# Output weights fetched ahead into lent ring places, convolution sums among the last projections, and triangular inverses by blocks of 64

## The chip, the cores and the metric

One core of one Trainium2 chip runs the kernel. The metric is the time of one execution on the device, in microseconds (us); the time before is the median of three runs, 1175.84 us (1175.05 to 1176.33). The engines are called PE (TensorE), PEld (its weight loads), DVE (VectorE), ACT (ScalarE), POOL (GpSimd) and SP (SyncE, which issues the loads).

## The reference

256 tokens of width 1024 go through two blocks. The first (Fourier mixing, neighbourhood attention, a gated merge and an MLP) is not touched. The second mixes three branches into one output projection and ends in 16 experts:

```python
h = rms_norm_2(x, norm_mix_g)
q, pc, pr = jnp.split(h @ w_in, ...)
o_att  = memory_cross_attention(q, mem_n, w_mk, w_mv)       # 256 wide
o_conv = conformer_conv(pc, conv_w, ...)                    # 384 wide, 31 taps in depth
o_rwkv = rwkv7_bidirectional(pr, ...)                       # 384 wide, 6 heads of 64
x = x + jnp.concatenate([o_att, o_conv, o_rwkv], -1) @ w_out
x = x + expert_choice_ffn(rms_norm_2(x, norm_ffn_g), w_router, w_e_gate, w_e_up, w_e_down)
return rms_norm_2(x, final_norm_g)

# each head, in both directions of time:
state = state * w_t + (state @ -kk_t) (kk_t * a_t)^T + v_t k_t^T
y_t   = state @ r_t
```

Each expert takes the 32 tokens of its highest gates. Its three matrices are 1024 x 1024 in float32, so the experts read 16 x 3 x 4 MB = 201 MB.

## The kernel before

**Block 2's branches** (`branches`) follow the last products of block 1. The input projections come first (`pw` <- `hmh`, `hml`: the activations as a high and a low half, times weights that ACT and DVE turn into a high and a low half, `split`). A projection piece is loaded by `wload` into a `raw` tile, split by `wsplit`, and multiplied by the generator that `dense_steps` returns.

**The recurrence without a scan.** The 256 steps are cut into two chunks of 128. `first_scores` and `other_scores` make each chunk's score matrices (`psab` on PE, masked into `LM` on DVE; `prh` and `py` carry the chunk's own values), for each direction twelve (6 heads, 2 chunks), held as three tiles `i` of four matrices `z`. A triangular system of 128 unknowns must then be inverted. `blocks16` inverts the 16x16 blocks on its diagonal (`prep` on PE, `g` and `Gc` on DVE, 15 rounds) and writes them into a 128x128 matrix `Gm`. `levels` doubles the blocks: 16 to 32, 32 to 64, and 64 to 128. A level needs the transposed inverse `Tm` (by `turn`: `pt`, copied by ACT), `pp` = score matrix times `Tm` (masked by DVE into `P`, in the last level copied by ACT), and `pg` = `P` times `Gm` (copied by ACT, in the last level by DVE). In the first two levels each of these is a 128x128 matmul with blocks of zeros in it; in the last it is 64x64, of one quadrant. `finish` then solves with the inverse (`pu`, `pzz`, `prz`, `py`). All of it is done for direction 0 and direction 1; direction 1's `blocks16` is woven among direction 0's levels.

**The convolution.** Two thirds of the channels are summed by DVE (`cacc`, one operation a tap). The last third is summed on PE: for each of the 31 taps ACT writes a scaled copy `cp` and PE adds it in with an identity (`pconv`, `conv_pe`). `conv` ends with the norm over channels (`pm` <- `cacc`, `aa`; a square root on ACT, RECIPROCAL on DVE, a sigmoid on ACT) and writes the high and low outputs `oc`. The memory attention's outputs are `om`, the recurrence's `orw`.

**The output projection** (`out_proj`) is cut by rows: `op` multiplies the 640 rows for attention and convolution by pieces of 256 columns, `second` the 384 rows for the recurrence by pieces of 512 columns, both added to `x`. The products of `op` are handed out by count among the steps of `finish(1)` (`OPB`) and of the tail behind it.

**The tail** norms the recurrence's output: `pm` <- `ysum`, squares, `pkk`, a square root, RECIPROCAL, `pbk`, products with the gate (`kds`), and at last `orw`.

**The ring.** The experts' weights go through places in SBUF in the order in which they are used (gate, up, down of expert 0, 1, ...): narrow places of 1 MB and wide ones of 2 MB. Places are added as memory comes free (`ring_room`), and `ring_load` issues into those that are free; `E1` says how many loads go where. Two of the last places serve for something else before: one as a `split` tile, one as `orw`.

**What sets the order.** Generators are woven by hand (`weave`, with the counts `W`), but each instruction recorded is then placed in its engine's queue by a scheduler, which may move it ahead of or behind others where nothing depends on it. `in_turn` holds it to the order of recording; all loads of block 2 on SP are held so. Each engine works its queue in order, so an instruction that waits holds up all behind it.

## Time and profile before

| | |
|---|---|
| median of 3 runs | 1175.84 us |
| the profiled execution | 1172.29 us, its span 1170.5 us |
| PE busy | 1046.5 us (89%) |
| DVE busy | 508.1 us (43%) |
| ACT busy | 418.2 us (36%) |
| DMA | 313.86 MB, 268 GB/s over the span |

The table is of one profiled execution; the median is of other runs. A share over the whole span is a mean over stages. Up to some 450 us block 1 runs, from there to 716 us block 2's branches, then the router and the experts. In the second part of the page the DMA row is at 9 (90% or more) from about 700 us to the end, with 426 to 428 GB/s, and at 0 to 4 before it; PE is at 9 up to there and at 7 to 8 behind. For a float32 matmul of the program the trace shows two on PE (8 in a level step of four matrices), for one on split halves (`pw`) one.

### The profile page before, as it was taken

What the parts mean: (1) busy time and instruction counts of PE and PEld (TensorE: products, weight loads), DVE (VectorE), ACT (ScalarE), POOL (GpSimd) and SP (SyncE); (2) the same over time, 40 slices, a digit from 0 to 9 for tenths busy, and PEclk for the clock granted to TensorE, in tenths of its full rate; (3) what the DMA queues carried; (4) which work ended last, traced back from release to release, by engine and by line L of the source; (5) the groups of instructions that cost most, each with busy time, mean ns of one, the idle gap of its engine ahead of it and who ended that gap; (6) DMA issues with size and microseconds to landing.
All of it is one profiled execution on the core that took longest, in us unless ns stands there. A gap on an engine that the chain in (4) does not pass through costs nothing.

```text
span 1170.5 us, 19106 instructions
## 1 busy us (share of the span) xinstructions
PE 1046.5 (89%) x8188; PEld 754.2 (64%) x8188; DVE 508.1 (43%) x964; ACT 418.2 (36%) x718; POOL 44.4 (4%) x50
## 2 busy tenths in 40 slices
PE   5999999999999999999899998989877777777775
PEld 4886676899999999898678887434332222222222
DVE  3544356587555555659997545212111111111102
ACT  4542368656444444676434534101100000000003
POOL 0000000021000000101210002000000000000000
PEclk9999999999999999999999998999988988998888
DMA  9974545545555553530401469999999999999996
GB/s 349 365 287 165 180 165 210 181 182 179 213 180 180 183 185 120 175 109 1 180 1 46 153 235 372 361 419 370 426 427 428 426 425 427 428 426 425 427 427 286
DMA packets 34964, 313.86 MB, mean 268 GB/s; under 512 B 4800, under 2 KB 5568, under 8 KB 9152
## 3 DMA queue, kind: packets, MB, share of 16 engines
q1 hardware_dynamic: 34880, 312.65, 67.2%
q8 instruction: 64, 1.05, 0.4%
q14 instruction: 20, 0.16, 0.0%
HBM read 311.59 MB, written 1.05 MB: 267 GB/s over the span
## 4 chain that ended last, share of the span: by engine, by line
PE 70%; DMA 20%; DVE 5%; ACT 3%; issue 1%; POOL 1%; SPq 0%; ACTq 0%; POOLq 0%; DVEq 0%
PE pw L299 22%; DMA ew<-in_w_e_up_dram 13%; PE pd L299 9%; PE acc L299 9%; DMA ew<-in_w_e_down_dram 6%; PE pgu L299 5%; PE pada L299 2%; PE pv L299 2%; PE pqf L299 2%; PE psab L299 2%; PE pg L299 1%; PE pconv L299 1%; PE pp L299 1%; PE py L299 1%; PE prep L299 1%; DMA raw<-in_w_branch_gate_dram 1%
## 5 line engine op out<-in xcount | busy, mean ns | idle before, releaser
L284 DVE TENSOR_TENSOR split<-raw,split 128x1024 fp32r<-128x1024 f32 (+2 forms) x148 | 176.8, 1203 | 114.2 <-ACT split L278 113.5
L299 PE MATMUL pgu<-ew,XE 128*32 128x256 f32 x2048 | 145.4, 427 | 57.2 <-DMA ew<-in_w_e_up_dram 56.0
L278 ACT ACTIVATE split<-raw 128x1024 fp32r<-128x1024 f32 (+2 forms) x148 | 151.9, 1033 | 123.8 <-PE pw L299 65.1
L299 PE MATMUL pd<-ew,hidT 128*32 128x512 f32 (+2 forms) x560 | 149.4, 572 | 12.4 <-DVE hidT L2137 6.2
L299 PEld LDWEIGHTS pgu<-ew,XE 128*32 128x32 f32 x2048 | 67.5, 120 | 127.3 <-DMA ew<-in_w_e_up_dram 68.9
L299 PEld LDWEIGHTS pd<-ew,hidT 128*32 128x32 f32 x560 | 40.5, 111 | 110.5 <-issue 97.3
L299 PE MATMUL acc<-uh,split 128*128 128x256 f32 x512 | 94.7, 283 | 0.0
L299 PE MATMUL pw<-h2h,split 128*128 128x256 f32 x512 | 92.9, 280 | 0.0
L296 DVE SCALAR_TENSOR_TENSOR hid<-pgu,rs,hid 128x256 f32<-128x256 f32 x16 | 7.7, 484 | 189.7 <-ACT hid L275 189.7
L296 DVE SCALAR_TENSOR_TENSOR ye<-pd,ig,ye 128x512 fp32r<-128x512 f32 (+2 forms) x35 | 24.6, 704 | 144.1 <-ACT ye L275 142.5
L275 ACT ACTIVATE hid<-pgu,rs 128x256 f32<-128x256 f32 x16 | 7.6, 474 | 215.0 <-PE pgu L299 215.0
L275 ACT ACTIVATE ye<-pd,ig 128x512 fp32r<-128x512 f32 (+2 forms) x35 | 22.8, 651 | 164.7 <-PE pd L299 164.6
L299 PEld LDWEIGHTS acc<-uh,split 128*128 128x128 f32 x512 | 80.8, 192 | 0.0
L299 PEld LDWEIGHTS pw<-h2h,split 128*128 128x128 f32 x512 | 79.3, 188 | 0.0
L299 PE MATMUL acc<-ul,split 128*128 128x256 f32 x256 | 72.5, 283 | 0.0
L299 PE MATMUL pw<-h2l,split 128*128 128x256 f32 x256 | 71.4, 279 | 0.0
L299 PE MATMUL pw<-hxh,split 128*128 128x256 f32 x320 | 61.6, 286 | 0.1
L299 PE MATMUL pw<-hmh,split 128*128 128x256 f32 x320 | 61.0, 288 | 0.0
L299 PEld LDWEIGHTS pw<-hxh,split 128*128 128x128 f32 x320 | 50.0, 188 | 9.5 <-issue 8.1
L299 PEld LDWEIGHTS pw<-hmh,split 128*128 128x128 f32 x320 | 50.5, 191 | 1.6 <-PE pz L299 0.5
L299 PEld LDWEIGHTS acc<-ul,split 128*128 128x128 f32 x256 | 49.0, 191 | 0.2 <-DVE ul L284 0.2
L299 PEld LDWEIGHTS pw<-h2l,split 128*128 128x128 f32 x256 | 48.0, 187 | 0.0
(441 smaller groups left out, 1734.0 us busy)
## 6 DMA issues: line engine op xcount, KB each, us to landing
ew<-in_w_e_up_dram SPq DMA_DIRECT2D x28, 2048.0 KB, 18.5
ew<-in_w_e_down_dram SPq DMA_DIRECT2D x28, 2048.0 KB, 19.1
ew<-in_w_e_gate_dram SPq DMA_DIRECT2D x27, 2048.0 KB, 22.5
raw<-in_w_mlp_dram SPq DMA_DIRECT2D x32, 1024.0 KB, 4.8
raw<-in_w_ada_dram SPq DMA_DIRECT2D x24, 1024.0 KB, 5.5
raw<-in_w_in_dram SPq DMA_DIRECT2D x18, 1024.0 KB, 5.7
ew<-in_w_e_gate_dram SPq DMA_DIRECT2D x10, 1024.0 KB, 12.9
raw<-in_w_branch_gate_dram SPq DMA_DIRECT2D x8, 1024.0 KB, 4.9
```

Of the source, the lines that this page charges most:

```text
L275: self.nc.scalar.activation(out, in_, func, **kw)
L278: self.nc.scalar.activation(out, in_, AF.Copy)
L284: self.nc.vector.tensor_tensor(out=out, in0=a, in1=b, op=op)
L296: self.nc.vector.scalar_tensor_tensor(out=out, in0=a, scalar=s, in1=b, op0=op0, op1=op1)
L299: self.nc.tensor.matmul(out, lhsT, rhs, start=start, stop=stop, **kw)
```

## The change

- `conv_pe` is made before the last projections and is handed out there: 4 taps among the last products and 8 after the first of the last steps, its copies in a tile of another pool.
- `Gm` and `Tm` hold the two 64x64 diagonal blocks, stacked over 128 partitions (128 x 4 x 64), instead of a 128x128 matrix. The levels 16 to 32 and 32 to 64 multiply 64x64 blocks on two diagonal quadrants of PE. The transposed inverse comes from its own product, `pt` = `P` times `Gm` the other way round, instead of a transposition of `pg`. Only before the last level is the inverse written out whole (`G`), with zeros by POOL.
- The 640 rows' pieces of `w_out` are loaded in one go as soon as memory is there: two into the two `raw` tiles, two into one lent wide ring place; the 384 rows' two pieces into another lent place. The first lent place goes back to the ring when `orw` is placed, the second when the output products are done. `E1` is gone; the ring loads what has room.
- The first pieces are split before direction 1's second level, and one step of `op` follows each of the last eight steps of that level and the last one.

```diff
 OPB = 5, 5, 5, 5, 0
-E1 = 4, 2, 2, 0
 PRE = 0
...
     out = []
+    def halves(m):
+        return np.concatenate([m[0:64, 0:64], m[64:128, 64:128]])
     for d in range(2):
...
             m = (r // (2 * n) == c // (2 * n)) & ((r // n) % 2 == 1) & ((c // n) % 2 == 0)
-            out.append(m | (s == t))
+            out.append(halves(m | (s == t)))
+    out.append(halves(s // 16 == t // 16))
     out.append(s // 16 == t // 16)
...
-    def wload(self, name, r0, r1, c0, c1, k=None):
-        wp, tag = self.raws[0]
-        self.raws = self.raws[1:] + self.raws[:1]
-        raw = wp.tile([128, 2048], F32, tag=tag, name="raw", bufs=1)
+    def wload(self, name, r0, r1, c0, c1, k=None, raw=None):
         src = self.wsrc(name, r0, r1, c0, c1)
+        if raw is None:
+            wp, tag = self.raws[0]
+            self.raws = self.raws[1:] + self.raws[:1]
+            raw = wp.tile([128, 2048], F32, tag=tag, name="raw", bufs=1)
         view = raw[:, 0:src.shape[1]]
...
                 self.branches(x2, hi, lo, ob)
-            self.ring_load()
             self.ring_room(RING2)
...
                     self.logits(x2, 2 * n - 2)
+            self.free.append(self.lent)
+            self.ring_load()
             with self.in_turn("PE"):
...
-    def out_proj(self, x, ob, h, between=0):
+    def out_proj(self, x, ob, h, piece):
...
         o = tuple(Tiles(lambda k, z=z: ob[a + k][:, z]) for z in range(2))
-        return self.dense_steps("w_out_2", 0, 1024, b - a, [o], [ev], preload=2, fine=not h,
-                                between=between and partial(self.ring_load, between), r0=a * 128)
+        return self.dense_steps("w_out_2", 0, 1024, b - a, [o], [ev], fine=not h, r0=a * 128, piece=piece)
...
+        cw = self.v("conv_w_2").rearrange("p (k i) -> p k i", k=31)
+        cacc = rb.tile([128, 3, 256], F32, name="cacc")
+        def conv_pe():
+            ps = self.pst("pconv")
+            for t in range(31):
+                p_ = self.sq.tile([128, 2, 256], F32, name="cp", tag="sq", bufs=2)[:, t % 2]
+                self.act(p_, u[:, 2, t:t + 256], AF.Copy, scale=cw[:, t, 2:3])
+                self.mm(ps[:, 0:256], self.ident, p_, t == 0, t == 30)
+                yield
+            self.act(cacc[:, 2], ps[:, 0:256], AF.Identity, bias=self.v("conv_b_2", 2))
+        cpe = conv_pe()
         dec, ky, s0, s1 = decays(), keys(), start(0), start(1)
...
         for g in (dec, cd, cd, dec, cd, ma, cd, dec, cd, ma, cd, None, prd, dec, prd, ma, prd, dec, prd, ma,
-                  ky, prd, ma, ky, s0, prd, s0, s0, prd, ma, s1, prd, s1, s1):
+                  ky, prd, ma, ky, s0, prd, s0, s0, prd, *[cpe] * 4, ma, s1, prd, *[cpe] * 8, s1, s1):
             if g is None:
...
         mst = [cr[:, 512 + d * 256:512 + (d + 1) * 256].rearrange("p (y t) -> p y t", y=2) for d in range(2)]
-        lev = [[cr[:, 1024 + (d * 2 + n) * 128:1024 + (d * 2 + n + 1) * 128] for n in range(2)] for d in range(2)]
+        lev = [[cr[:, 1024 + (d * 2 + n) * 64:1024 + (d * 2 + n + 1) * 64] for n in range(2)] for d in range(2)]
         bm = cr[:, _CR["bm"]:_CR["bm"] + 128]
+        bmh = cr[:, _CR["bmh"]:_CR["bmh"] + 64]
         sel = wk2.tile([128, 2064], F32, name="sel")
...
-        def conv_pe():
...
-                p_ = wk2.tile([128, 256], F32, name="cp", tag="cp", bufs=2)
...
                [matrices(i) for i in range(3, 6)]]
-        gms = itertools.cycle([(wk if n in (1, 2, 3) else wk0).tile([128, 4, 128], F32, name="Gm%d" % n)
-                               for n in range(7)])
+        whole = [[p.tile([128, 4, 128], F32, name="G%d%d" % (d, n)) for n in range(3)] for d, p in enumerate((wk0, wk))]
+        gms = itertools.cycle([wk0.tile([128, 4, 64], F32, name="Gm%d" % n) for n in range(9)])
...
                 gm = G[d, i] = next(gms)
-                self.tt(gm.rearrange("p n (b c) -> p n b c", b=8),
-                        g[:, 4 * i:4 * i + 4, None, :].to_broadcast([128, 4, 8, 16]),
-                        bm.rearrange("p (b c) -> p b c", b=8)[:, None].to_broadcast([128, 4, 8, 16]), ALU.mult)
+                self.tt(gm.rearrange("p n (b c) -> p n b c", b=4),
+                        g[:, 4 * i:4 * i + 4, None, :].to_broadcast([128, 4, 4, 16]),
+                        bmh.rearrange("p (b c) -> p b c", b=4)[:, None].to_broadcast([128, 4, 4, 16]), ALU.mult)
             yield
-            turn(d)
+            for i in range(3):
+                turned(d, i, [self.ident[q, None, q].to_broadcast([64, 4, 64]) for q in hs])
             yield
+        hs = slice(0, 64), slice(64, 128)
         def v4(ps):
-            return ps.rearrange("p (n t) -> p n t", n=4)
-        def turn(d):
+            return ps[:, 0:256].rearrange("p (n t) -> p n t", n=4)
+        def turned(d, i, factors, which=hs):
+            ps = v4(self.pst("pt1", "pw"))
+            for z in range(4):
+                for q in which:
+                    self.mm(ps[q, z], G[d, i][q, z], factors[hs.index(q)][:, z], True, True)
+            T_[d, i] = wk0.tile([128, 4, 64], F32, tag="Tm", name="Tm", bufs=3)
+            for q in (which if len(which) == 1 else [slice(0, 128)]):
+                self.cpa(T_[d, i][q], ps[q])
+        def levels(d):
+            a, b = hs if d == 0 else hs[::-1]
             for i in range(3):
-                ps = v4(self.pst("pt1", "pw"))
-                for z in range(4):
-                    self.tr(ps[:, z], G[d, i][:, z])
-                T_[d, i] = wk0.tile([128, 4, 128], F32, tag="Tm", name="Tm", bufs=3)
-                self.cpa(T_[d, i], ps)
-        def levels(d):
+                nc.gpsimd.memset(whole[d][i][b, :, a], 0.0)
             for n in range(2):
-                ml = lev[d][n][:, None, :].to_broadcast([128, 4, 128])
+                ml = lev[d][n][:, None, :].to_broadcast([128, 4, 64])
                 p1 = []
...
                     for z in range(4):
-                        self.mm(ps[:, z], LM[d, i][:, 0, z], T_[d, i][:, z], True, True)
-                    t = wk0.tile([128, 4, 128], F32, tag="P1", name="P1", bufs=3)
+                        for q in hs:
+                            self.mm(ps[q, z], LM[d, i][q, 0, z, q], T_[d, i][q, z], True, True)
+                    t = wk0.tile([128, 4, 64], F32, tag="P1", name="P1", bufs=3)
                     p1.append(t)
...
                     for z in range(4):
-                        self.mm(ps[:, z], p1[i][:, z], G[d, i][:, z], True, True)
-                    G[d, i] = next(gms)
-                    self.cpa(G[d, i], ps)
+                        for q in hs:
+                            self.mm(ps[q, z], p1[i][q, z], G[d, i][q, z], True, True)
+                    turned(d, i, [p1[i][q] for q in hs], [a] if n else hs)
+                    if n == 0:
+                        G[d, i] = next(gms)
+                        self.cpa(G[d, i], ps)
+                    else:
+                        G[d, i] = whole[d][i]
+                        for q in hs:
+                            self.cpa(G[d, i][q, :, q], ps[q])
                     yield
-                turn(d)
-                yield
-            a, b = (slice(0, 64), slice(64, 128)) if d == 0 else (slice(64, 128), slice(0, 64))
             p1 = []
             for i in range(3):
-                ps = self.pst("pp1", "pw").rearrange("p (n t) -> p n t", t=64)
+                ps = v4(self.pst("pp1", "pw"))
                 for z in range(4):
-                    self.mm(ps[b, z], LM[d, i][a, 0, z, b], T_[d, i][a, z, a], True, True)
-                t = wk0.tile([128, 4, 128], F32, tag="P1", name="P1", bufs=3)
+                    self.mm(ps[b, z], LM[d, i][a, 0, z, b], T_[d, i][a, z], True, True)
+                t = wk0.tile([128, 4, 64], F32, tag="P1", name="P1", bufs=3)
                 p1.append(t)
-                self.cpa(t[b, :, 0:64], ps[b, 0:4])
+                self.cpa(t[b], ps[b])
                 yield
             for i in range(3):
-                ps = self.pst("pg1").rearrange("p (n t) -> p n t", t=64)
+                ps = v4(self.pst("pg1"))
                 for z in range(4):
-                    self.mm(ps[a, z], p1[i][b, z, 0:64], G[d, i][b, z, b], True, True)
-                self.cpv(G[d, i][a, :, b], ps[a, 0:4])
+                    self.mm(ps[a, z], p1[i][b, z], G[d, i][b, z, b], True, True)
+                self.cpv(G[d, i][a, :, b], ps[a])
                 yield
...
                 yield from g
-        cpe, late, bon, f0 = conv_pe(), other_scores(1), bonus(), finish(0)
+        late, bon, f0 = other_scores(1), bonus(), finish(0)
         weave(first_scores(0), (cpe, W[0]))
...
         self.wmore(self.es, "wps", 0, 2)
-        parts, ready = iter(self.out_proj(x2, ob, 0)), collections.deque()
+        rows0, rows1 = {}, {}
+        for c in (0, 256):
+            rows0[c] = self.wload("w_out_2", 0, 640, c, c + 256)
+        parts, ready = iter(self.out_proj(x2, ob, 0, rows0)), collections.deque()
...
         op = products()
-        self.go(lv)
+        prepare(2)
+        for n, _ in enumerate(lv):
+            if n < 8:
+                next(op)
         brief.close()
...
         self.free.reverse()
-        self.ring_load(E1[0])
-        prepare(3)
+        lent = [p for p in self.free if p in self.wide][:2]
+        for p in lent:
+            self.free.remove(p)
+        for (pool, tag), got, r0, r1, c0, n in zip(lent, (rows0, rows1), (0, 640), (640, 1024), (512, 0), (256, 512)):
+            t = pool.tile([128, 2, 2048], F32, tag=tag, name="raw", bufs=1)
+            for z in range(2):
+                c = c0 + z * n
+                got[c] = self.wload("w_out_2", r0, r1, c, c + n, raw=t[:, z])
+        self.ring_load()
+        prepare(1)
         fin = finish(1)
...
             if n == 3:
-                self.ring_load(E1[1])
                 self.act(sm.tile([128, 1], F32, name="root"), aa[1][:, 0, 128:129], AF.Sqrt, scale=0.0, bias=self.eps6)
...
         ob.extend(orw[:, :, i] for i in range(3))
-        self.free.extend(late[2:])
-        self.ring_load(E1[2])
         prepare()
-        second = self.out_proj(x2, ob, 1, E1[3])
+        self.free.append(lent[0])
         self.ring_load()
+        second = self.out_proj(x2, ob, 1, rows1)
+        self.lent = lent[1]
         self.dbg("ysum", ysum)
```

**SP, the loads from the projections to the second expert.** `w_out` is the output projection, `ew` a ring place; 128x4096 is 2 MB, 128x1536 is 768 KB. Before:

```order
L1913 DMA ew<-in_w_e_gate_dram 128x2048 x4
L335 DMA raw<-in_w_out_dram 128x1280 x2
L1913 DMA ew<-in_w_e_up_dram 128x4096 x2
L335 DMA raw<-in_w_out_dram 128x1280
L1913 DMA ew<-in_w_e_down_dram 128x4096
L335 DMA raw<-in_w_out_dram 128x1280
L1913 DMA ew<-in_w_e_down_dram 128x4096
L335 DMA raw<-in_w_out_dram 128x1536 x2
L1913 DMA ew<-in_w_e_gate_dram 128x4096 x2
```

And with the change:

```order
L1938 DMA ew<-in_w_e_gate_dram 128x2048 x4
L340 DMA raw<-in_w_out_dram 128x1280 x4
L340 DMA raw<-in_w_out_dram 128x1536 x2
L1938 DMA ew<-in_w_e_up_dram 128x4096 x2
L1938 DMA ew<-in_w_e_down_dram 128x4096 x2
L1938 DMA ew<-in_w_e_gate_dram 128x4096 x2
```

All six loads of `w_out` now stand ahead of up of expert 0. In the program's semaphores the first of them waits for the last `py` of the scores and the last write of its `LM`; the second half of down of expert 0 waits for the last `orw`.

**PE, the end of direction 1's levels.** `pp`, `pg` and `pt` are the steps of a level, `pw` the output products, `pu` the first step of `finish`. Before:

```order
L299 MATMUL pg_6723<-Gm_5778,P_6695 128x128 x4
L299 MATMUL pg_6729<-Gm_5779,P_6714 128x128 x4
L299 MATMUL pg_6735<-Gm_5773,P_6721 128x128 x4
L303 MATMUL pt_6741<-cm,Gm_5774 128x128 x4
L303 MATMUL pt_6748<-cm,Gm_5775 128x128 x4
L303 MATMUL pt_6755<-cm,Gm_5776 128x128 x4
L299 MATMUL pp_6762<-Tm,LM_5770 64x64 x4
L299 MATMUL pp_6769<-Tm,LM_5771 64x64 x4
L299 MATMUL pp_6776<-Tm,LM_5772 64x64 x4
L299 MATMUL pg_6783<-Gm_5774,P_6767 64x64 x4
L299 MATMUL pw<-om,split 128x256 x3
L299 MATMUL pg_6789<-Gm_5775,P_6774 64x64 x4
```

And with the change:

```order
L303 MATMUL py_6816<-LM_6770,vtok 64x128 x3
L303 MATMUL pp_6867<-Tm,LM_5809 64x64 x8
L303 MATMUL pg_6882<-Gm_5816,P_6836 64x64 x8
L303 MATMUL pg_6903<-Gm_5817,P_6847 64x64 x8
L303 MATMUL pg_6924<-Gm_5818,P_6876 64x64 x8
L303 MATMUL pw<-om,split 128x256 x3
L303 MATMUL pt_6891<-P_6836,Gm_5816 64x64 x4
L303 MATMUL pw<-om,split 128x256 x3
L303 MATMUL pt_6912<-P_6847,Gm_5817 64x64 x4
L303 MATMUL pw<-oc,split 128x256 x3
L303 MATMUL pt_6933<-P_6876,Gm_5818 64x64 x4
L303 MATMUL pw<-oc,split 128x256 x3
```

The first `pw` stood behind all `pt` and `pp` of the last level; now it stands ahead of them, and the products alternate with the level's steps (eight such rounds). Up to the first `pu` there are 30 products where there were 10, and 36 instead of 60 are left behind the variance (`pm` <- `ysum`).

**DVE, where the convolution's norm ends.** `aa` is the root of the variance, `LM` the last score matrices, `ysum` the sum of outputs. Before:

```order
L284 TENSOR_TENSOR rh_5761<-rh_5761,prz 128x3x64 x2
L1509 RECIPROCAL aa_5045<-aa_5045 128x256
L284 TENSOR_TENSOR LM_6561<-psab,cr 128x2x2x128
L284 TENSOR_TENSOR cacc<-cacc,aa_5045 128x768
L284 TENSOR_TENSOR LM_6561<-psab,cr 128x2x2x128
```

And with the change:

```order
L288 TENSOR_TENSOR ysum<-ysum,py 128x512
L288 TENSOR_TENSOR ysum<-ysum,py 128x256
L1508 RECIPROCAL aa_5045<-aa_5045 128x256
L288 TENSOR_TENSOR LM_6770<-psab,cr 128x2x2x128
L288 TENSOR_TENSOR cacc<-cacc,aa_5045 128x768
L288 TENSOR_TENSOR LM_6770<-psab,cr 128x2x2x128
```

The RECIPROCAL stood ahead of the sums of direction 0's outputs, among the score matrices before the last; now it stands behind those sums and ahead of the last score matrices.

## Rows read from the trace of the kernel before

**Rows 1.** Page, chain that ended last: shares of the span by line
```profile
PE pw L299 22%; DMA ew<-in_w_e_up_dram 13%; PE pd L299 9%; PE acc L299 9%; DMA ew<-in_w_e_down_dram 6%; PE pgu L299 5%; PE pada L299 2%; PE pv L299 2%; PE pqf L299 2%; PE psab L299 2%; PE pg L299 1%; PE pconv L299 1%; PE pp L299 1%; PE py L299 1%; PE prep L299 1%; DMA raw<-in_w_branch_gate_dram 1%
```

**Rows 2.** Windows: length, then PE, PEld, DVE, ACT, POOL busy, PE clock, DMA, GB/s
```profile
730.00:760.00 30.00, 29.04 (x285) 13.86 (x281) 6.49 (x19) 4.94 (x8) 0.00 (x0) 1.00 0.94 363
900.00:930.00 30.00, 22.31 (x173) 8.73 (x172) 3.95 (x8) 2.60 (x5) 0.00 (x0) 0.94 1.01 426
```

**Rows 3.** SP's loads: start us, us, count; then loads of 640 to 704, KB, landing
```profile
628.79 4.57 SPq L335 DMA_DIRECT2D raw<-in_w_out_dram  x2
704.17 0.88 SPq L1913 DMA_DIRECT2D ew<-in_w_e_gate_dram  x2
735.08 5.72 SPq L1913 DMA_DIRECT2D ew<-in_w_e_gate_dram  x3
...
ew<-in_w_e_up_dram SPq DMA_DIRECT2D x2, 2048.0 KB, 8.9
ew<-in_w_e_down_dram SPq DMA_DIRECT2D x2, 2048.0 KB, 9.5
```

**Rows 4.** Windows by stage, the same columns as rows 2
```profile
569.40:605.30 35.90, 35.69 (x185) 25.02 (x184) 30.82 (x77) 13.89 (x32) 6.63 (x5) 1.00 0.06 23
605.30:631.10 25.80, 25.51 (x221) 24.00 (x222) 24.06 (x72) 11.81 (x24) 1.39 (x1) 1.00 0.06 17
631.10:676.50 45.40, 45.37 (x382) 37.36 (x383) 26.34 (x49) 20.96 (x40) 0.00 (x0) 1.00 0.39 151
```

**Rows 5.** PE in direction 0's levels: start, us, instruction, count
```profile
612.04 0.49 PE L299 MATMUL prep<-N,sel 128*128 128x192 f32 x2
612.37 1.05 PE L299 MATMUL pg<-Gm,P 128*128 128x128 f32 x8
613.26 0.49 PE L299 MATMUL prep<-N,sel 128*128 128x192 f32 x2
...
627.57 0.68 PE L299 MATMUL pp<-Tm,LM 64*64 64x64 f32 x8
628.17 0.59 PE L299 MATMUL prep<-N,sel 128*128 128x192 f32 x2
628.69 0.97 PE L299 MATMUL pp<-Tm,LM 64*64 64x64 f32 x13
...
629.55 0.22 PE L299 MATMUL pg<-Gm,P 64*64 64x64 f32 x1
629.56 0.22 PE L299 MATMUL pp<-Tm,LM 64*64 64x64 f32 x1
...
629.67 1.38 PE L299 MATMUL pg<-Gm,P 64*64 64x64 f32 x21
```

**Rows 6.** DVE: the block writes of direction 0, the convolution's RECIPROCAL
```profile
605.31 1.88 DVE L284 TENSOR_TENSOR Gm<-Gc,cr 128x512 f32<-128x512 f32 x3
...
647.70 1.75 DVE L1509 RECIPROCAL aa<-aa 128x256 f32<-128x256 f32 x1 [0.42 <-ACT aa L275]
```

**Rows 7.** PE from the last py to pu, and the products on orw
```profile
664.54 0.66 PE L303 MATMUL pt<-cm,Gm 128*128 128x128 f32 x4
...
673.66 0.61 PE L299 MATMUL pw<-om,split 128*128 128x256 f32 x3
...
674.81 0.51 PE L299 MATMUL pw<-om,split 128*128 128x256 f32 x2
...
676.54 0.55 PE L299 MATMUL pu<-rh,Gm 128*128 128x64 f32 x4
...
703.78 4.46 PE L299 MATMUL pw<-orw,split 128*128 128x256 f32 x36
```

**Rows 8.** A load of w_out (KB, us to landing) and its halves on ACT and DVE
```profile
raw<-in_w_out_dram SPq DMA_DIRECT2D x2, 640.0 KB, 4.4
...
665.73 0.73 ACT L278 ACTIVATE split<-raw 128x640 fp32r<-128x640 f32 x1
...
668.52 0.81 DVE L284 TENSOR_TENSOR split<-raw,split 128x640 fp32r<-128x640 f32 x1
```

23 lines of the change are left out of this document (4 added, 19 removed).

## The prediction

> **What bounds the kernel now.** I read the chain of waits first. Its line shares put 19% of the span on the landing of expert weights (`ew`) and most of the rest on TensorE [rows 1]. The windows say where each holds: in 900 to 930 us the DMA engines are full, 426 GB/s, while TensorE is busy 22.3 of 30 us [rows 2]. So behind the router the kernel is a stream of 201 MB, and what was streamed early is what it doesn't stream there.
>
> Then the list of SyncE's instructions. Only 12 MB of expert weights are on their way before 704.17 us: 4 MB of gate (not touched by the change), two issues of up and two of down of 2 MB each [rows 3]. The issue at 704.17 waits for `orw`, the last write into a borrowed ring place, made by the branch's last VectorE product. I call that moment E; products on it run from 703.78 [rows 7]. From E the stream runs behind, so the end is E plus the bytes left over 426 GB/s plus the stream's own holes. In 730 to 760 us it moved 363 GB/s [rows 2]: 30 x (1 - 363/426) = 4.4 us are lost there, because the ring is full and SyncE waits for an expert's places (the next issue is at 735.08 [rows 3]).
>
> Before E the windows by stage show two limits [rows 4]. From 569.4 to 605.3 VectorE works 30.8 of 35.9 us; from 605.3 to 631.1 TensorE and VectorE are both near full (25.5 and 24.1 of 25.8); afterwards TensorE alone (45.4 of 45.4).
>
> **The change part by part**, as shifts of E in us (minus is earlier).
>
> 1. Convolution's sums in the projections. Ten more of the 31 taps, two matmuls each, leave the VectorE-bound stretch, and seven of VectorE's own tap operations come into it. Its idle time is 5.1 us [rows 4], the most that can be won; seven operations on 128x256, each under the 0.63 of one on 128x512 [rows 6], are the most that can be lost, 4.4. I take -0.5, near no change, since idle time and new work about cancel. In the projections the taps stand behind the memory softmax on ScalarE, so TensorE waits there; VectorE has its own queue to work off, so I put nothing.
>
> 2. Blocks of 64, first direction (605.3 to 631.1). A level step of 128 columns takes 613.26 - 612.37 = 0.89, the `prep` between two of them 0.33. The old last level shows what 64x64 blocks cost: eight matmuls with their neighbour 0.60 and a `prep` among them 0.52 [rows 5]. Starts there are 0.058 apart (21 in 1.38 with 0.22 for the last), so eight alone are 0.46; a `prep` among small blocks thus adds 0.14 + 0.19 = 0.33 for the two changes of shape. Sixteen matmuls on two diagonal quadrants take 0.46 as well if the two run side by side; where `pp` and `pg` of different quadrants meet, they start at the same moments [rows 5], so I take that. New sum: 27 steps of 0.46, 13 `prep` of 0.33, 13 alternations of 0.33 make 21.0. The first block write (three operations, 1.88 [rows 6]) halves to about 1.1. Together 22.1, with 0.4 for waits 22.5, against 25.8: -3.3. VectorE's floor is close: six masks and three block writes lose about 0.27 of their 0.63 each, an estimate for half the columns: 24.1 - 2.4 = 21.7.
>
> 3. Second direction up to its last scores. By the same prices the nine steps and the turn there gain 0.5. But the convolution's RECIPROCAL (1.75 [rows 6]) now stands in VectorE's queue behind the sum of the first direction's outputs and ahead of the last score masks (the order of VectorE shows it), and the last `prh`, `py` wait for those; about half of it shows, as VectorE has idle time there: +0.8. Sum +0.3.
>
> 4. Output products among the last steps. In the order before, `pw` stands behind the last `pp`; now the first `pw` stands ahead of the last turns and of everything behind it on TensorE. Its weights are the first `w_out` load. That was issued at 628.79 [rows 3]; in the new program its semaphores are those of the last score matrices and of the last `py`, because the raw tile now lies where those were. So: issue 0.2 after the last `py`, landing 4.4, ScalarE's half 0.73, VectorE's 0.81 [rows 8], 6.15 in all, in which TensorE has four small steps (1.8) and otherwise nothing. Then eight rounds of three products and one block step. The old program has such a round: 674.81 - 673.66 = 1.15 [rows 7]. 8 x 1.15, another block step 0.46 and six products at 4.46/36 = 0.124 make 10.4. From the last `py` to the first `pu` that is 16.5 where it was 676.54 - 664.54 = 12.0 [rows 7]: +4.5. If the wait and the rounds overlapped wholly it would be -1; if the splits queue behind the convolution's last operations, +7.
>
> 5. The rest up to E. Between `pu` and the variance four more products, +0.5. In the tail 24 products are gone from TensorE, but VectorE's chain (variance, RECIPROCAL, gate, sums) decides there; one split joins it and two leave ahead of it, 0.8 each way [rows 8]: 0.
>
> 6. Lending. E then waits for less of the ring: 10 MB instead of 12 are loaded before it (the second half of down of expert 0 goes behind `orw`). 2.1 MB at 426 GB/s are 4.9 us more to stream. Against it stand the 4.4 us of holes: with 14 MB queued at E instead of 12, the queue is still working when the old one ran dry. +0.5, bounds 0 and +4.9.
>
> Sum: -0.5 - 3.3 + 0.3 + 4.5 + 0.5 + 0 + 0.5 = +2.0. The profiled execution took 1172.3; 1174.3 in its terms. The median of the runs shown, 1175.84, lies 3.55 above it, so 1177.8; I write 1177.5, as the holes may be filled wholly.
>
> **A rule that speaks against the change.** The Trainium skill, page "TensorEngine Tiling (Array Packing)", section "Key Properties", says that changing the tiling mode drains TensorE, while tiles of one mode work independently and in parallel. The trace agrees with both halves: 0.14 and 0.19 per change, 0.32 for the two in a round with `pw` (1.15 - 0.46 - 3 x 0.124), and the paired starts [rows 5, 7]. By the first half every alternation in points 2 and 4 pays, as in the sum; if the gaps were only waits for copies, the first rival holds.
>
> **Rivals.**
> - The changes of shape cost nothing in longer runs. For: in the rows of point 4 ScalarE and VectorE also evacuate between the steps. Against: the gap is the same in every round. Then 13 alternations lose 4.3 but VectorE's floor of 21.7 keeps point 2 at -4.1; point 3 gains 2, the eight rounds 8 x 0.33 = 2.6, and in point 1 the idle goes, -2: sum 2.0 - 0.8 - 2.0 - 2.6 - 1.5 = -4.9, time 1171.
> - The quadrants don't run side by side. For: the old steps use only one at a time, the pairs in [rows 5] are few and belong to different steps. Then 18 steps of point 2 cost 0.46 more each (8.3), and the eleven of point 3 ahead of the wait 5.1: +13, about 1190. It decides once a step of 16 takes over 0.62: 18 x 0.62 + 9 x 0.46 + 13 x 0.66 = 23.9, TensorE's time there now (25.8 less the block writes' 1.9).
> - The holes at 730 to 760 stay, because they come from places that come free late and not from a dry queue. For: SyncE waits there for TensorE's release of a place. Against: 14 MB last 34 us, past the release at 735.08. Then point 6 is +4.9 and the time 1182.
>
> **Numbers.** Forecast 0.44, its own range 1174 to 1182 (points 1, 2 and 4 by about 2 each). Free changes of shape 0.32, serial quadrants 0.13, holes stay 0.11. What a measurement of this kernel can't tell from no change is 0.2%, 2.35 us: 1173.5 to 1178.2. The forecast gives same 0.26, slower 0.16, faster 0.02; the first rival faster 0.28 and same 0.04; the others slower 0.24. Faster 0.30, same 0.30, slower 0.40. The range reaches to the first rival with its uncertainty (1168) and upwards past the third, part of the way into the second (1187).
>
> **What would show it.** Right: the first `w_out` issue right behind the last `py`, TensorE idle some 4 us ahead of its first `pw` <- `om`; `pw` x3 and block steps alternating at 1.1 to 1.2; a `pp` of 16 matmuls in about 0.46; DMA at full rate through 733 and 753. Wrong: a `pw` that starts without a wait (point 4), steps of 0.9 (second rival), `prep` 0.33 among small blocks (first rival), a window 730 to 760 well under 426 GB/s (third). The forecast falls if `orw` is written more than 3 us earlier or later than about 705.3.

## The result, and the profile after

The changed kernel takes 1192.1 us (median of four runs, 1186.9 to 1193.2), the kernel before 1175.4 beside it: ratio 1.0141, 95% interval 1.0117 to 1.0165. Slower by 16.7 us, where 1177.5 and a range up to 1187 were forecast. The profiled execution took 1192.24 with a span of 1190.1, 19.6 more than the one before. Cut at events that both traces have, that splits so (us; E is the moment of the gate issue right behind `orw`):

| stretch | before | after | difference | forecast |
|---|---|---|---|---|
| start to the first `pu` of direction 0 (points 1, 2) | 631.0 | 632.7 | +1.7 | -3.8 |
| to the last score `py` of direction 1 (3) | 33.0 | 32.8 | -0.2 | +0.3 |
| to the first `pu` of direction 1 (4) | 12.6 | 24.4 | +11.8 | +4.5 |
| to E (5) | 27.6 | 32.3 | +4.6 | +0.5 |
| E to the end (6) | 466.3 | 468.0 | +1.6 | +0.5 |

The third line is three fifths of it. The first line does not measure points 1 and 2: up to that `pu` six of the runs below are the same program as the changed kernel, and their traces reach it anywhere from 628.2 to 633.9 us.

TensorE in the third line, in the changed kernel (start, us, instruction, count, idle time before it and what ended it), against the last four of [rows 7]:

```profile
665.48 0.65 PE L303 MATMUL py<-LM,vtok 128*64 128x128 f32 x6
...
666.98 1.61 PE L303 MATMUL pg<-Gm,P 64*64 64x64 f32 x48 [0.24 <-DVE P L288]
672.52 0.59 PE L303 MATMUL pw<-om,split 128*128 128x256 f32 x3 [3.92 <-DVE split L288]
673.03 0.76 PE L303 MATMUL pt<-P,Gm 64*64 64x64 f32 x8
673.72 1.01 PE L303 MATMUL pw<-om,split 128*128 128x256 f32 x3
674.66 1.11 PE L303 MATMUL pt<-P,Gm 64*64 64x64 f32 x8
675.70 1.01 PE L303 MATMUL pw<-oc,split 128*128 128x256 f32 x3
...
689.88 0.95 PE L303 MATMUL pu<-rh,G 128*128 128x64 f32 x4
```

The idle time ahead of the first `pw` is there, 3.92 us. But a round, from one `pw` to the next, takes 1.98 us (675.70 - 673.72), not the 1.15 of [rows 7]. The reason stands in a column that the prediction never used, the granted clock (the figure before the DMA share; 0.50 is 1.2 GHz, 1.00 is 2.4). First the kernel before over three stretches (last `py` to `pu`, on to the variance, and from the first `pw` on `orw`), then the changed kernel, with short windows at the end:

```profile
664.50:676.50 12.00, 12.00 (x124) 11.27 (x123) 6.16 (x10) 6.42 (x13) 0.00 (x0) 1.00 0.95 385
676.50:692.90 16.40, 16.40 (x149) 13.42 (x147) 4.56 (x9) 5.31 (x9) 0.00 (x0) 1.00 0.60 233
703.80:729.50 25.70, 21.60 (x156) 18.54 (x154) 15.39 (x42) 10.42 (x23) 7.16 (x7) 0.81 0.95 390
```

```profile
666.06:689.88 23.82, 19.66 (x167) 16.77 (x167) 7.97 (x15) 10.02 (x21) 0.00 (x0) 0.66 0.69 272
689.88:709.62 19.74, 19.74 (x152) 16.83 (x151) 5.53 (x9) 5.71 (x9) 0.00 (x0) 0.81 0.24 98
720.20:748.45 28.25, 22.01 (x155) 18.64 (x155) 13.43 (x40) 9.88 (x23) 7.15 (x7) 0.82 0.92 377
...
670.00:672.00 2.00, 0.00 (x0) 0.00 (x0) 1.55 (x4) 2.00 (x5) 0.00 (x0) 1.00 1.00 389
672.00:674.00 2.00, 1.48 (x12) 1.26 (x13) 1.10 (x2) 0.69 (x3) 0.00 (x0) 0.87 1.03 417
674.00:676.00 2.00, 2.00 (x12) 1.66 (x13) 0.00 (x0) 0.34 (x2) 0.00 (x0) 0.50 1.01 415
686.00:696.00 10.00, 10.00 (x70) 9.34 (x69) 2.51 (x5) 1.23 (x2) 0.00 (x0) 0.50 0.56 210
696.00:698.00 2.00, 2.00 (x13) 1.98 (x12) 0.36 (x1) 0.36 (x1) 0.00 (x0) 0.65 0.00 0
```

TensorE stands idle, and from about 673.7 to 697 it runs at half clock, although it is then busy without a gap (10.00 of 10.00). The kernel before has 1.00 in its first two stretches.

The other stages are the counterpart of [rows 3, 5, 6]. SyncE's issues: `w_out` right behind the last `py`, all six pieces at once; E 18.0 us later than 704.17; the next gate issue.

```profile
666.16 6.10 SPq L340 DMA_DIRECT2D raw<-in_w_out_dram  x6
...
722.15 1.96 SPq L1938 DMA_DIRECT2D ew<-in_w_e_gate_dram  x2
...
753.90 5.73 SPq L1938 DMA_DIRECT2D ew<-in_w_e_gate_dram  x3
```

Direction 0 on TensorE, and the block writes on VectorE that it waits for:

```profile
608.80 2.82 PE L303 MATMUL pt<-cm,Gm 64*64 64x64 f32 x48 [3.63 <-DVE Gm L288]
...
616.11 0.68 PE L303 MATMUL pg<-Gm,P 64*64 64x64 f32 x16
616.62 0.63 PE L303 MATMUL pt<-P,Gm 64*64 64x64 f32 x16
617.19 0.59 PE L303 MATMUL prep<-N,sel 128*128 128x192 f32 x2
617.71 0.68 PE L303 MATMUL pg<-Gm,P 64*64 64x64 f32 x16
```

```profile
607.72 1.69 DVE L288 TENSOR_TENSOR Gm<-Gc,cr 128x256 f32<-128x256 f32 x3
```

A step `pg` is 0.51 and the `prep` after a step 0.52: the blocks do run side by side and the changes of shape cost what was forecast. Here too a wait (3.63 us) is followed by half clock, 608.8 to about 612.

One and the same wait need not bring the clock down every time. Ahead of the first `prep` TensorE waits 1.39 us in the changed kernel; in e8_products_later below, which is the same program up to there, it waits as long. Each wait with the window behind it, the changed kernel first:

```profile
580.83 1.20 PE L303 MATMUL prep<-N,sel 128*128 128x192 f32 x4 [1.39 <-DVE N L1562]
...
582.00:592.00 10.00, 10.00 (x51) 8.08 (x49) 6.33 (x21) 3.10 (x8) 0.00 (x0) 0.69 0.00 1
```

```profile
578.78 0.92 PE L303 MATMUL prep<-N,sel 128*128 128x192 f32 x4 [1.39 <-DVE N L1562]
...
580.00:590.00 10.00, 10.00 (x70) 7.69 (x70) 8.95 (x29) 4.58 (x11) 0.00 (x0) 1.00 0.01 2
```

Of the seven traces with this program the clock fell there in four, which reach the first `pu` of direction 0 at 631.5 to 633.9 us, and held in three, which reach it at 628.2 to 630.1.

The expert stream, against [rows 2]: the holes are filled, 415 GB/s for 363.

```profile
748.00:778.00 30.00, 29.04 (x272) 13.87 (x275) 6.49 (x19) 5.41 (x9) 0.00 (x0) 0.99 1.01 415
900.00:930.00 30.00, 21.33 (x186) 8.11 (x176) 3.20 (x7) 1.85 (x3) 0.00 (x0) 0.93 1.01 427
```

### The profile page after: what moved, and what is told of

It reads as the page before. It is cut to its first block, busy times and chain, and to the rows that moved or that the text cites. A ratio compares the mean times of both kernels' runs of the same rounds, so it can differ in the third digit from the quotient of the medians.

```text
span 1190.1 us, 19836 instructions
## 1 busy us (share of the span) xinstructions
PE 1054.3 (89%) x8548; PEld 756.2 (64%) x8548; DVE 504.9 (42%) x964; ACT 414.8 (35%) x724; POOL 47.2 (4%) x56
## 4 chain that ended last, share of the span: by engine, by line
PE 68%; DMA 19%; DVE 6%; ACT 4%; issue 1%; POOL 1%; SPq 0%; ACTq 0%; POOLq 0%; DVEq 0%
PE pw L303 23%; PE pd L303 11%; DMA ew<-in_w_e_down_dram 10%; PE acc L303 9%; DMA ew<-in_w_e_up_dram 8%; PE pgu L303 5%; PE pv L303 2%; PE pada L303 2%; PE py L303 1%; DVE split L288 1%; PE prep L303 1%; PE pqf L303 1%; PE pt L303 1%; ACT split L282 1%; DMA raw<-in_w_branch_gate_dram 1%; PE pp L303 1%
## 5 line engine op out<-in xcount | busy, mean ns | idle before, releaser
L303 PE MATMUL pgu<-ew,XE 128*32 128x256 f32 x2048 | 142.9, 422 | 55.7 <-DMA ew<-in_w_e_up_dram 55.1
L303 PE MATMUL pd<-ew,hidT 128*32 128x512 f32 (+2 forms) x560 | 153.3, 589 | 12.7 <-DMA ew<-in_w_e_down_dram 6.9
## 6 DMA issues: line engine op xcount, KB each, us to landing
ew<-in_w_e_gate_dram SPq DMA_DIRECT2D x10, 1024.0 KB, 10.9
```

Source lines behind the costliest of these rows:

```text
L303: self.nc.tensor.matmul(out, lhsT, rhs, start=start, stop=stop, **kw)
```

## The experiments

Theory A: TensorE's idle time ahead of the first `pw` brings the clock down, and the slow clock is most of the loss. B: the 64x64 matmuls of the new levels bring it down. C: products between block steps cost 2 us a round by themselves. D: the moved sums are the cost. Every ratio is to the kernel before, timed on the same chip, with its 95% interval; "changed" is the kernel of the diff.

**First set: the load, the idle time, the sums, the order.** One line keeps 2 KB in the early pool, so that the first raw tile lies elsewhere:

```diff
         sel = wk2.tile([128, 2064], F32, name="sel")
+        wk2.tile([128, 512], F32, name="spare")
```

> The changed kernel with 2 KB left unused in the early pool, so that the raw tiles of the first two w_out pieces no longer lie over LM1; their loads then wait for prep and for Gm8 of the second direction, both done before 640, not for the last py at 665.5. Nothing else differs. Theory A (the late first load idles TensorE for 3.9 us ahead of the first pw, and the granted clock then stands at 0.50 until 696, so that a round costs 1.98 us in place of 1.15): no wait ahead of the first pw, clock 1.0 over 666 to 697, rounds near 1.15; 3.9 and 8 x 0.83 = 6.6 us and some 2 us of the last products come back: 1179 to 1181. Rival B (the 64x64 matmuls of the new levels are what brings the clock down): only the wait goes, the clock stays at 0.50: about 1188. Rival C (products between the steps of the levels cost 1.98 a round by themselves, by changes of shape): also about 1188, with the clock at 1.0.

1189.2 us, 1.0101 (1.0068 to 1.0135), not A's 1179 to 1181. The loads were issued at 628, and still `pw` waited:

```profile
664.24 1.61 PE L303 MATMUL pg<-Gm,P 64*64 64x64 f32 x48 [0.24 <-DVE P L288]
669.78 0.98 PE L303 MATMUL pw<-om,split 128*128 128x256 f32 x3 [3.92 <-DVE split L288]
```

ScalarE in the same run shows why: the split stands in its queue behind five `G` and the three `oc` that end the convolution, without a gap.

```profile
665.30 1.93 ACT L282 ACTIVATE G<-pg 64x256 f32<-64x256 f32 x5
667.13 1.02 ACT L282 ACTIVATE oc<-cacc 128x256 fp32r<-128x256 f32 x3
668.05 1.35 ACT L282 ACTIVATE split<-raw 128x640 fp32r<-128x640 f32 x2
```

So the late load, which the prediction and theory A named as the cause of the wait, was not what ended it. The clock fell as before, which decides nothing between A and B.

The next run leaves the wait and fills it:

```diff
         for n, _ in enumerate(lv):
+            if n == 0:
+                with self.in_turn("PE"):
+                    ps = self.pst("pm")
+                    for _ in range(7):
+                        self.mm(ps[:, 0:256], self.ident, x2[:, 0], True, True)
             if n < 8:
```

> The changed kernel with seven unused fp32 matmuls of 128x256 (about 0.43 us each, 3.0 us in all) between the last pp and the first pg of the last level steps; the first w_out load stays late, at the last py. Theory A in its clock part: TensorE is no longer idle while the piece lands, the clock stays at 1.0, the rounds cost 1.15 though the first pw still starts near 672.5: about 8 us less than the change, 1183 to 1185. If only the wait matters and the clock is brought down by something else (B): the clock still falls to 0.50 and the time is that of the change or up to 1 us more, 1192 to 1193. Rival C: the same 1192.

1177.9 us, 1.0020 (0.9995 to 1.0044): 3 us of useless work make the kernel 14 us faster, more than A's 8. The first `pw` starts no earlier, the rounds take 1.15, the clock stays at 1.00:

```profile
667.67 3.29 PE L303 MATMUL pm<-x,cm 128*128 128x256 f32 x14
670.89 1.61 PE L303 MATMUL pg<-Gm,P 64*64 64x64 f32 x48
672.81 0.62 PE L303 MATMUL pw<-om,split 128*128 128x256 f32 x3 [0.30 <-DVE split L288]
673.36 0.68 PE L303 MATMUL pt<-P,Gm 64*64 64x64 f32 x8
673.96 0.62 PE L303 MATMUL pw<-om,split 128*128 128x256 f32 x3
```

A window of the same run (columns as above):

```profile
674.00:684.00 10.00, 10.00 (x99) 8.59 (x98) 3.38 (x6) 4.62 (x11) 0.00 (x0) 1.00 1.03 421
```

C falls with this run. So does the thought that the traffic brings the clock down: the DMA engines move 421 GB/s in this window, at 1.00.

The sums back among the blocks (`conv_pe` where it was, its tiles in `wk2`, no `cpe` in the projections' list):

> The changed kernel with the convolution's sums on TensorE back among the blocks (no taps in the last projections, the products' tiles in the early pool again); the early pool thereby has its 2 KB back, and the first two w_out loads are early as in the first run. Theory A: the time of the first run less or plus what the taps cost in the projections: they take 1.5 us ahead of the first pt (608.8 for 607.3), and come back among the blocks with 31 x about 0.11 us of slots there, so within 2 us of the first run: 1178 to 1182. Rival D (the moved sums are what cost): the first run stays above 1188 and this one falls to about 1178.

1192.4 us, 1.0146 (1.0089 to 1.0204): D falls. The expectation of 1178 to 1182 came from the early load, which does not help.

The products behind the last level steps again, as in the kernel before:

```diff
-        prepare(2)
-        for n, _ in enumerate(lv):
-            if n < 8:
-                next(op)
+        self.go(lv)
...
-        prepare(1)
+        prepare(3)
```

> The changed kernel with the output products behind the last level steps again (three pieces split there, as before); the first w_out load stays late, at the last py. Theory A: the levels need no piece, the first direction-1 pu comes 12 us after the last py, not 23.8, TensorE has no wait of 3.9 us and the clock stays at 1.0 there; the eight rounds then stand behind pu beside the state products as before, and the time is near that of the kernel before less the 0.2 to 2 us of filled holes: 1174 to 1180. If A's clock part is wrong and the clock falls from the 64x64 matmuls (B): clock at 0.50 in the level steps, 1184 or more.

1173.1 us, 0.9967 (0.9947 to 0.9986), just under A's 1174 to 1180. Yet the clock is not at 1.00, as A had it: there is a wait of 0.91 us for ScalarE's `Tm` between the last two `pp`, and half clock from 675 to 684. That wait is filled in the fourth set.

**Second set: each part alone, and the products later.** The kernel before with the levels, constants and block writes of the diff alone:

> The kernel before with the inverses by blocks of 64 alone (no moved sums, no lent places, products behind the levels). The prediction had -3.3 us for them in the first direction and +0.3 up to the last scores. The changed kernel's trace has 23.9 us from the first pt to the first pu of that direction, against 23.7 before, so if that holds without the other parts the first direction gives nothing, and only the last steps of the second give about 2.5 us (10.1 from the last py to its pu in the run with the products behind, 12.6 before): 1173 to 1174 with 1176 for the kernel before. If the prediction's term was right and another part ate it: 1171 to 1172.

1177.7 us, 1.0013 (0.9993 to 1.0033): no gain, above both expectations. The same wait of 0.91 us stands in it, and half clock from 676 to 682. With the sums' part of the diff alone:

> The kernel before with the convolution's sums in the last projections alone. The prediction had -0.5 us. If the sums cost what the changed kernel's trace shows up to the first pt of direction 0 (1.5 us later): +1 to +2 us, 1177 to 1178 with 1176 for the kernel before; if the taps that leave the blocks give this back there: 1175 to 1176.

1172.7 us, 0.9976 (0.9959 to 0.9992): a gain, larger than either expectation. With the lent places alone, products behind:

> The kernel before with the w_out pieces in lent ring places alone (the first pieces' loads and the order of the products as before). The prediction had +0.5 us, for 1.0 us of later stream and 4.4 us of filled holes in it. The changed kernel has 415 GB/s over 748 to 778, in place of 363 over 730 to 760, and its end is 0.7 us later against the step that frees the last gate; by that about 1175 to 1177 with 1176 for the kernel before. If the filled holes count in full: 1172.

1173.5 us, 0.9983 (0.9965 to 1.0000), between its two expectations. The changed kernel with `if n > 3` in place of `if n < 8`:

> The changed kernel with the products' rounds begun four steps later among the last level steps (six rounds there in place of eight): the three transposes' products pt now stand ahead of the first pw. In the changed kernel TensorE stood idle 3.9 us ahead of that pw, though the pt had all they need; 1.7 us of the idle time is filled so, and 2.2 us stay, in which the pp wait for ScalarE's Tm behind the oc and the split. Theory A (idle time, whatever ends it, brings the clock down; the wait is for ScalarE's and VectorE's queue, not for the load): if 2.2 us of idle time are too little for the clock to fall, it stays at 1.0, and the time is that of the run with a busy wait or less, 1173 to 1178; if it falls all the same, 1186 to 1190. Rival C (products among the levels cost by themselves): 1186 or more with the clock at 1.0.

1179.9 us, 1.0041 (1.0021 to 1.0061). The wait was 2.17 us, and the clock fell all the same, from 670 to 684:

```profile
667.96 0.62 PE L303 MATMUL pw<-om,split 128*128 128x256 f32 x3 [2.17 <-DVE split L288]
```

The time is between the expectations: the slow stretch is shorter than the 24 us of the changed kernel.

**Third set: a wait where the 64x64 blocks are not.** The kernel before, with GpSimd as the brake:

```diff
-        self.go(lv)
+        for n, _ in enumerate(lv):
+            if n == 1:
+                d = LM[0, 0].rearrange("p a n t -> p (a n t)")[:, 0:512]
+                self.tp(d, T_[1, 0].rearrange("p n t -> p (n t)"), d, ALU.add)
+                for _ in range(4):
+                    self.tp(d, d, d, ALU.subtract)
+                with self.in_turn("PE"):
+                    ps = self.pst("pm")
+                    self.mm(ps[:, 0:256], self.ident, d[:, 0:256], True, True)
```

> The kernel before, with five operations on GpSimd (otherwise idle there, 1.3 to 1.9 us each) started by ScalarE's Tm near 663.5 and one unused matmul on TensorE that reads the last of them, ahead of the pg at 667.7: TensorE is made to stand idle 3 to 5 us there, in the levels of 128 columns and with the products behind. Theory A (idle time on TensorE at this place brings the granted clock to 0.50, whatever is beside it): the clock, 1.0 there in the kernel before, falls to 0.50 for 8 us or more behind the wait, and the time grows by the wait and by 4 us or more: 1183 to 1190, with 1175 for the kernel before. Rival B (it takes the 64x64 matmuls of the new levels): the clock stays at 1.0 and only the wait is added, 1178 to 1180.

1178.2 us, 1.0017 (1.0002 to 1.0031). The wait came out at 1.67 us, half of what was meant, and the clock stayed at 1.00: B's time and clock as expected, but with too short a wait to judge A.

```profile
673.36 0.70 PE L299 MATMUL pm<-LM,cm 128*128 128x256 f32 x2 [1.67 <-POOL LM L287]
```

The window behind it:

```profile
676.00:680.00 4.00, 3.97 (x52) 3.56 (x51) 0.83 (x1) 3.82 (x9) 0.00 (x0) 1.00 0.96 397
```

With `range(6)` for `range(4)`:

> The kernel before with two more of the GpSimd operations than in the earlier run with a forced wait (1.1 us each there), so that TensorE stands idle some 3.9 us ahead of the pg in the levels of 128 columns, as long as in the changed kernel ahead of its first pw. If idle time of that length is enough by itself, the clock falls to 0.50 behind it and the time is 4 us or more above the shorter wait's 1178 plus 2: 1184 to 1190. If it also takes the 64x64 matmuls around it (the theory as the runs so far leave it), the clock stays at 1.0 and only the 2.2 us are added: 1179 to 1181.

1182.5 us, 1.0057 (1.0040 to 1.0074). Now the wait was 4.83, and the clock fell among matmuls of 128 columns:

```profile
674.42 1.22 PE L299 MATMUL pm<-LM,cm 128*128 128x256 f32 x2 [4.83 <-POOL LM L287]
```

The window behind it:

```profile
676.00:680.00 4.00, 4.00 (x21) 4.00 (x20) 0.00 (x0) 1.51 (x3) 0.00 (x0) 0.50 0.87 270
```

B as the only cause falls: idle time is enough. The time is below A's 1184, as this slow stretch lasts only 7 us. The counterpart fills the changed kernel's wait with the very matmuls that B accuses, `self.mm(ps[q, z], self.ident[q, q], x2[q, 0, z * 64:z * 64 + 64], True, True)` 48 times:

> The changed kernel with its wait filled by 48 unused matmuls of 64x64 in two quadrants (about 3 us, the kind that the new levels are made of) in place of the seven of 128x256 in the run with the busy wait. If an idle TensorE is what brings the clock down, it stays at 1.0 and the time is that run's, 1177 to 1179. If the light 64x64 work counts like idle time, the clock falls to 0.50 as in the changed kernel and the time is the change's, 1190 to 1193.

1179.1 us, 1.0035 (1.0009 to 1.0061), the time expected if idle time is the cause, and a round 1.15 again:

```profile
665.31 2.97 PE L303 MATMUL pm<-x,cm 64*64 64x64 f32 x96
670.51 0.62 PE L303 MATMUL pw<-om,split 128*128 128x256 f32 x3 [0.83 <-DVE split L288]
671.66 0.62 PE L303 MATMUL pw<-om,split 128*128 128x256 f32 x3
```

The window behind it:

```profile
674.00:684.00 10.00, 10.00 (x104) 8.86 (x105) 4.45 (x7) 4.26 (x9) 0.00 (x0) 1.00 1.00 391
```

And the changed kernel with levels of 128 columns:

> The changed kernel with the inverses of 128 columns as before, and the products among their last steps; the first w_out load is early here or late by the pools, and the first pw stands behind the oc and the split on ScalarE as in the changed kernel. If a wait of about 4 us ahead of that pw is enough by itself: the clock falls to 0.50 behind it, rounds near 2 us, 1184 to 1190. If it takes the 64x64 matmuls too: the clock stays at 1.0 and the time is that of the moved sums and lent places (1172) plus the wait and the emptier tail, 1176 to 1180.

1179.3 us, 1.0034 (1.0014 to 1.0055), the clock 1.00 behind the first `pw`, as B had it. But here the broader steps fill the time themselves and only 1.28 us of wait are left, so it does not tell A from B. It shows that products among the steps cost 6 to 7 us over products behind (1172.5, below) even at full clock.

**Fourth set: the gaps filled.** Three unused matmuls in the 0.91 us of the run with the products behind:

```diff
-        self.go(lv)
+        for n, _ in enumerate(lv):
+            if n == 4:
+                with self.in_turn("PE"):
+                    ps = self.pst("pm")
+                    for _ in range(3):
+                        self.mm(ps[:, 0:256], self.ident, x2[:, 0], True, True)
```

> The run with the products behind the levels (moved sums, lent places, blocks of 64), with three unused matmuls of 0.43 us in the 0.9 us that TensorE waits for ScalarE's Tm between the last two pp. In that run the clock was at 0.50 from about 675 to 684, right behind that wait. Theory A: the clock stays at 1.0 there; some 4 us of the slower stretch come back less 0.4 us of delay: 1169 to 1170. Rival B (the 64x64 matmuls): the clock falls all the same, and the time stays at 1173 or 0.4 us above it.

1169.1 us, 0.9951 (0.9935 to 0.9968): faster than both kernels, and the best here. First the wait and the window in the run without the three matmuls, then the same two views with them:

```profile
674.36 1.04 PE L303 MATMUL pp<-Tm,LM 64*64 64x64 f32 x8 [0.91 <-ACT Tm L282]
```

```profile
674.00:684.00 10.00, 9.49 (x58) 8.95 (x59) 3.73 (x7) 4.34 (x11) 0.00 (x0) 0.52 1.03 423
```

```profile
667.60 1.56 PE L303 MATMUL pm<-x,cm 128*128 128x256 f32 x6
669.09 1.14 PE L303 MATMUL pp<-Tm,LM 64*64 64x64 f32 x16
```

```profile
674.00:684.00 10.00, 10.00 (x110) 9.42 (x109) 4.61 (x8) 3.17 (x6) 0.00 (x0) 1.00 1.02 433
```

The same three matmuls with the blocks of 64 alone:

> The kernel before with the blocks of 64 alone and the three unused matmuls in the wait for Tm between the last two pp. With the blocks alone the time was 1.0013 of the kernel before, and its clock was at 0.50 from about 675 to 682, some 3.5 us lost. If that is what ate their gain: clock at 1.0 there, 0.9975 to 0.9985 of the kernel before, 1172 to 1174 with 1176. If the blocks give nothing by themselves: 1.001 again.

1172.3 us, 0.9972 (0.9955 to 0.9989), the clock 1.00 behind them: the blocks are worth 3.3 us (1.3 to 5.3 by the interval), and the slow clock had eaten it. Six unused matmuls in the wait ahead of the `pw` on `orw`, on top of the busy wait:

> The run with the busy wait (products among the last level steps, seven unused matmuls), with six more unused matmuls in TensorE's wait of 2.0 us ahead of the first pw of the second half (those that read orw), where no product is left to fill it; the clock was at 0.57 for 4 us behind that wait. Theory A: the clock stays at 1.0, and the stretch from the first of these pw to the first pgu, 28.3 us, shrinks by about 2 us to the 26 of the kernels with products left there: 1175 to 1176. If that clock is brought down by something else: 1178.

1178.3 us, 1.0023 (1.0008 to 1.0039). The clock behind that wait was 1.00, where the busy-wait run has 0.57 for 712 to 716, and the stretch to the first `pgu` went from 28.3 to 26.6 us, as A said. The time did not fall to A's 1175 to 1176; the two intervals overlap, so 1.7 us can't be told here. And the sums and lent places without the blocks:

> The moved sums and the lent places together, with the inverses as in the kernel before and the products behind the last steps. The single runs gave 0.9976 and 0.9983 of the kernel before; if the two add, as different stages suggest (the projections and the experts' stream), 0.996, 1170 to 1171 with 1175 for the kernel before, and faster than both kernels. With the blocks of 64 beside them it was 0.9967.

1172.5 us, 0.9979 (0.9966 to 0.9993): faster than before, but not the 0.996 of two gains that add.

## Why the prediction was wrong

The step that failed is in point 4: "Then eight rounds of three products and one block step. The old program has such a round: 674.81 - 673.66 = 1.15". That price was read at a granted clock of 1.00 and used behind a wait of some 4 us that the same point had forecast. The wait came, the clock behind it was 0.50, and the rounds took 1.98. With the wait filled they take 1.15, and last `py` to first `pu` is 16.9 us in the busy-wait run and 16.8 in the light-fill one, for 12.6 before: +4.3, for the +4.5 forecast. The rest of the +11.8, 7.5 us, is the clock, shown by the two fills.

No rival spoke of it. The trace of before offered it: in 703.8 to 729.5, shown above, TensorE is idle 4.1 of 25.7 us and the clock is 0.81. The Trainium skill, page "TensorE: Matmul & The Clock Gate", section "A second HAM failure mode: psum-queue depth-cycling", says that a TensorE which idles often enough for short moments between groups of matmuls swings between its two clocks. The traces agree in part: behind 0.91 us of idle time among the new levels the clock was 0.50 for some 9 us, but that was one wait and not many.

Point by point:

1. Sums, -0.5. Alone they gave 0.9976, some -2.8: the sign was right, the size too small. The gain lies ahead of the first `pt` of direction 0, which starts at 606.8 us on average in the eleven traces with the sums moved (603.6 to 610.1) and at 610.1 in the seven without (607.3 to 611.9). From there to E the run with the sums alone takes 96.5 us, for 96.9 before, although its first `pt` waits 3.90 us for VectorE where taps stood before, as it waits 3.63 in the changed kernel.
2. Blocks, -3.3 in the first direction. The prices were right (`pg`, `pt` and `prep` together 1.60, for 1.58), the place was not: alone the stage from first `pt` to `pu` takes 24.0 us at clock 1.00, for 23.7. There were 15 `prep` between steps, not 13 (two more are 1.3), and three taps of the convolution. The gain is in the last steps of the second direction: from the last `py` to `pu` 8.9 with the blocks alone and the wait filled, for 12.6. Of it 1.2 is lost again up to the variance (17.5 for 16.3), where the products stand that were ahead of `pu`. That the sum, 3.3 once the clock holds, came out as forecast is luck.
3. Up to the last scores, +0.3: measured -0.2.
4. The wait of 6.15 from the last `py`: measured 6.4, by another queue: the splits stood behind the convolution's last operations on ScalarE. The prediction had named that case as its upper bound, +7; the early load did not shorten the wait. The condition named there, a `pw` behind its load, looked confirmed in the trace, since both ended within a microsecond; only moving the load told them apart.
5. +0.5: measured +4.6. 3.4 is the clock, still at 0.50 up to 697 (19.7 from `pu` to the variance, for 16.4 in the busy-wait run and 16.3 before; so the +0.5 for four more products does not show either). The other 1.2 is the tail from the variance to E, 12.5 for 11.3, costed at 0. The run with the lent places alone has 12.5 too, so this belongs to the lending. Between the RECIPROCAL and `orw` VectorE has two splits of 768 columns there (0.95 each), one in the kernel before, and none in the run with the products later, where the tail takes 10.8: the split that joins is on the path, the two that leave ahead of it were not.
6. Lending, +0.5: the holes were filled as forecast (the third rival is out). E to the end takes 465.2 to 466.1 us in the six traces with lent places whose clock stays at 1.00 behind the first `pw` on `orw`, and 466.3 to 469.3 in the six without lending, on average 1.6 more. The 468.0 of the changed kernel holds the slow clock behind the wait ahead of that `pw`; with the wait filled it is 466.1. With the 1.2 of the tail the lending is worth about -0.4, and its times say 0.9983 (up to 1.0000): at the edge of what can be told.

So 10.9 of the 19.6 us between the two profiled executions are the clock in points 4 and 5. By the times of the two fills, ratios 1.0020 and 1.0035 for 1.0141, it is 12 to 14 us, of 16.7. With the wait filled the changed kernel stands at 1178 to 1179, where the forecast was 1177.5, but two of its errors cancel there: blocks that gain elsewhere, sums and lending that gain more, against products among the steps that cost more than +4.5. Against the same kernel with products behind they cost 8 to 10 us (1177.9 and 1179.1 for 1169.1). The traces of the busy-wait run and of that one put 6.8 of it between the last `py` and E and 2.4 behind E, where no product is left for the wait ahead of the first `pw` on `orw`. The forecast had set its new order against the old levels (12.0), not against the faster ones (8.9 from `py` to `pu`, for 16.9).

What stays open: which short waits bring the clock down. Waits of 1.3 and 1.7 us among steps of 128 columns, and of 0.8 us behind the light fill, left it at 1.00, and 0.9 us among the 64x64 steps did not; but each is one trace or two, and the 1.39 us ahead of `prep` went both ways. Open too is why the slow stretch lasts 24 us in the changed kernel and 7 behind the longest wait of all, and whether the fills hold the clock every time. One of ten executions with the busy wait took 1185.9 us and two of ten with the light fill 1185.6 and 1187.8, at a mean granted clock of 0.947 to 0.951, where the others had 0.954 to 0.965; of these three there is no trace.

## What to carry to other kernels

A duration from a trace holds for the clock it was read at. Where a change puts a wait ahead of TensorE's work, look in the same trace at the granted clock behind the waits that are already there, and price the work behind the new wait at half clock as a rival of its own. And a wait that the profile puts down to one engine can have a second queue that ends at the same moment: take the supposed cause away alone before building on it, and try unused matmuls in the gap, which here were worth 12 to 14 us. Where the clock can fall or hold, one trace of a kernel is a sample: compare a stage over several.

## What the runs showed of the hardware

- A TensorE that is busy without a gap stayed at 0.50: 686 to 696 in the changed kernel, 10.00 of 10.00 us busy, in rounds of three `pw` and eight 64x64 matmuls. The same rounds run at 1.00 where no wait stands ahead of them. So the slow clock outlasted the wait by some 24 us here.
- What fills the gap matters little: 3.3 us of 128x256 matmuls (1177.9 us) or 3.0 us of 64x64 ones (1179.1) both kept 1.00 in the executions traced.
- The price of the slow clock can exceed the wait that brings it: 3.92 us of idle time went with 10.9 us lost behind it, 0.91 with 4.0 (43.0 from the last `py` to E without the three unused matmuls, 39.0 with them).
- A wait of 1.39 us in the same program brought 0.50 behind it in four executions of seven and left 1.00 in three.
- 64x64 matmuls on two diagonal quadrants run side by side: sixteen in the trace's count take 0.51 from start to start of the next, eight took 0.46 by the spacing in [rows 5].
